# First block row tile by row tile, conditioning summed on VectorE, weights packed in order of use

## The chip, the core and the metric

The kernel runs on one core of a Trainium2 chip. The metric is the time of one execution on the device in microseconds; several runs are made, and their median counts. TensorE multiplies matrices from SBUF into PSUM, VectorE (DVE), ScalarE (ACT) and GpSimd (POOL) work on tiles of 128 partitions, and SyncE (SP) issues the transfers.

## The reference, cut to what matters

Two layers over 512 tokens of width 1024, each with a token mixer and a gated FFN. Every sub-layer is conditioned on a vector `c`:

```python
cs = jax.nn.silu(c)
for layer in range(DEPTH):
    mod = jnp.matmul(cs, ada_w[layer]) + ada_b[layer]          # 1024 x 6144
    sh_m, sc_m, g_m, sh_f, sc_f, g_f = split(mod, 6)
    h = rmsnorm(x, norm_mix_g[layer]) * (1 + sc_m) + sh_m
    y = even_mixer(h, ...) if layer % 2 == 0 else odd_mixer(h, ...)
    x = x + g_m * y
    h = rmsnorm(x, norm_ffn_g[layer]) * (1 + sc_f) + sh_f
    x = x + g_f * conv_glu_ffn(h, ...)
return rmsnorm(x, final_g)
```

The even mixer projects h by a 1024 x 3584 matrix into HGRN2 heads and stick-breaking heads, the odd one by 1024 x 3088 into mLSTM heads, and each has an output projection. Everything is float32.

## The kernel before

x lies transposed in SBUF, 8 row tiles of 128 features by 512 tokens. Each weight and each activation is split into two rounded parts (hi and lo), and a product is three matmuls: hi by hi, hi by lo, lo by hi (`mm3`). `load_split` issues one transfer per weight block from the weight as it lies in memory, casts it to hi on ScalarE and subtracts on VectorE for lo.

Conditioning: `ada_chunk` handles 512 columns of `ada_w` at a time. Its 1024 rows come in four pieces of 512 KB; VectorE multiplies each 128 rows by their value of `cs` and adds them up (8 operations over 128x512). `ada_close` then transposes the sum on TensorE (four transposes, 128x128) and VectorE sums it over the partitions. All chunks but the first four, which the first block handles on its own, are spread over later stages by generators (`ada_many`).

First block (`even_layer`, L536 on): the products with columns 3072 to 3584 and 2560 to 2816 of `even_w_in` (6 outputs) are made first, by quarters q of the features (two row tiles each). For a quarter, `conditioning(q)` loads 8 pieces of 256 KB and adds them up with 8 VectorE operations, `conditioned(q)` makes eight small matmuls with a vector of ones, the gains, and `modulate` (two VectorE and one ScalarE operation per row tile) gives h; `w_load` splits the weights, with the subtraction on GpSimd (`pool_lo`). `products(q, pass)` makes the matmuls of one pass.

After the first block, `weave` runs the chains of the heads step by step with dense products (`cover`) between the steps. Norms: `Stat.add` squares each updated row tile on ScalarE and adds the squares on GpSimd; `ssq_of` sums them over the partitions with matmuls by ones, `rstd_of` takes the power on GpSimd and spreads the result with transposes. This is done for each half of the tokens at the end of a sub-layer, inside `halves_out`, whose second half is multiplied while the first half's h is made.

The order on each engine is set by a list scheduler that goes by program order and its own estimates of when an operand is ready; `behind()` holds a small operation behind the last product queued. All tiles of the `work` pool are shared by all stages, 45 of them.

Of the kernel before, what the change touches and what calls it, by code (L numbers as in the profile page):

```python
# [36 lines left out]

@with_exitstack
def trunk(ctx: ExitStack, tc: tile.TileContext, xT, par_d, masks_d, ada_w, even_w_in, even_w_out,
          odd_w_in, odd_w_out, ffn_w_in, ffn_w_out, outT):  # L40
    nc = tc.nc
    NW, NR, NS, NA = 45, 2, 3, 3
# [65 lines left out]
    nc.vector.tensor_mul(cs, cs, pc("c", 0, 8))  # L108

# [7 lines left out]
    # ---------------- conditioning  # L117
    def ada_chunk(layer, cb):
        a = wt("adaacc")
        before = ada_open[:]  # L120
        del ada_open[:]
        for k2 in range(4):
            r = adap.tile([P, 2, T], F32, tag="ada", name=nm("adaraw"))
            nc.sync.dma_start(r, ada_w[layer, k2 * 256:(k2 + 1) * 256, cb * 512:(cb + 1) * 512]
                              .rearrange("(k p) c -> p k c", p=P))
            for i2 in range(2):
                k = k2 * 2 + i2
                if k == 0:
                    nc.vector.tensor_scalar(a, r[:, 0, :], cs[:, 0:1], None, op0=ALU.mult)
                else:  # L130
                    nc.vector.scalar_tensor_tensor(a, r[:, i2, :], cs[:, k:k + 1], a, op0=ALU.mult, op1=ALU.add)  # L131
            if k2 == 3 and before:
                ada_open.extend(before)
                ada_close()
            yield 0
        ada_open.append((layer, cb, a))

    ada_open = []

    def ada_close():  # L140
        while ada_open:
            layer, cb, a = ada_open.pop(0)
            ps = ps_mx()
            for j in range(4):
                nc.tensor.transpose(ps[:, j * P:(j + 1) * P], a[:, j * P:(j + 1) * P], ident)  # L145
            o = layer * 48 + cb * 4
# [4 lines left out]
    def ada_many(layer, chunks):  # L151
        for cb in chunks:
            yield from ada_chunk(layer, cb)
# [977 lines left out]
```

## Time and profile before

| | |
|---|---|
| median of 3 runs | 1317.85 us (1317.41 to 1317.86) |
| span of the profiled execution | 1316.1 us, 16372 instructions |
| median less the span | 1.75 us |
| TensorE busy | 1271.8 us (97%) |
| VectorE busy | 811.6 us (62%) |
| ScalarE busy | 466.6 us (35%) |
| GpSimd busy | 178.1 us (14%) |
| DMA | 162.51 MB, mean 123 GB/s |

The profile covers one execution from its first to its last instruction; the time of a run also holds what lies outside that. A matmul's duration includes its way through the array, so a stream of them starts every 0.23 us or so though each lasts 0.39.

### The profile page before, as it was taken

The numbers are of one execution on the slowest core, as the hardware profiler recorded it, in microseconds if no ns is written. First come the engines' busy times: TensorE is split into PE (matmuls) and PEld (weight loads), VectorE is DVE, ScalarE is ACT, GpSimd is POOL, SyncE is SP. The second block draws the span as 40 slices with busy tenths as digits, with TensorE's granted clock in tenths as the row PEclk, the third lists the DMA queues.
The fourth block names the chain that finished last, engine by engine and source line by source line (L and its number), as shares of the span: only waits on it lengthen the run. The fifth ranks groups of instructions, "written<-read, shape, count | busy, mean of one in ns | idle before, by whom it ended". The sixth has DMA issues, their size and how long they took to land.

```text
span 1316.1 us, 16372 instructions
## 1 busy us (share of the span) xinstructions
PE 1271.8 (97%) x6458; PEld 1053.1 (80%) x6458; DVE 811.6 (62%) x1198; ACT 466.6 (35%) x725; POOL 178.1 (14%) x258
## 2 busy tenths in 40 slices
PE   4899999999999999999999999999999999999997
PEld 3677788889888888888898768778988888888887
DVE  6844368996797368835756865666785435443454
ACT  3354313124432123212245674775532213221321
POOL 1322144414000000000031020113300000000012
PEclk9999999999999999999999999999999999999998
DMA  8741143562476247633433312112152222222221
GB/s 261 254 154 64 64 129 125 164 192 97 140 234 203 95 150 233 201 119 113 152 113 97 127 33 96 65 65 65 65 184 88 97 95 96 96 97 96 80 72 65
DMA packets 132717, 162.51 MB, mean 123 GB/s; under 512 B 4896, under 2 KB 102944, under 8 KB 132640
## 3 DMA queue, kind: packets, MB, share of 16 engines
q1 hardware_dynamic: 132640, 161.46, 37.8%
q8 instruction: 51, 0.84, 0.3%
q14 instruction: 26, 0.21, 0.1%
HBM read 159.35 MB, written 2.10 MB: 123 GB/s over the span
## 4 chain that ended last, share of the span: by engine, by line
PE 86%; DVE 5%; issue 4%; POOL 2%; ACT 2%; DMA 1%; SPq 0%; POOLq 0%; DVEq 0%; ACTq 0%
PE acc L189 19%; PE acc L190 19%; PE acc L191 19%; PE mx L189 5%; PE mx L190 5%; PE mx L191 5%; PE mx L418 2%; PE acc L227 1%; PE acc L225 1%; PE acc L226 1%; PE mx L808 1%; PE mx L834 1%; PE mx L463 1%; POOL sqa L247 1%; PE mx L145 1%
## 5 line engine op out<-in xcount | busy, mean ns | idle before, releaser
L190 PE MATMUL acc<-hl,wah 128*128 128x512 f32 (+1 forms) x384 | 144.2, 377 | 1.1 <-DVE hl L310 1.0
L189 PE MATMUL acc<-hh,wah 128*128 128x512 f32 (+1 forms) x384 | 145.0, 378 | 0.0
L191 PE MATMUL acc<-hh,wgl 128*128 128x512 f32 (+1 forms) x384 | 144.3, 376 | 0.0
L191 PE MATMUL acc<-hh,wal 128*128 128x512 f32 (+1 forms) x384 | 144.1, 376 | 0.0
L189 PE MATMUL acc<-hh,wgh 128*128 128x512 f32 (+1 forms) x384 | 144.1, 375 | 0.0
L190 PE MATMUL acc<-hl,wgh 128*128 128x512 f32 (+1 forms) x384 | 144.0, 375 | 0.0
L178 DVE TENSOR_TENSOR wl<-wraw,wh 128x2048 fp32r<-128x2048 f32 (+1 forms) x41 | 89.9, 2192 | 54.2 <-ACT wh L177 54.2
L177 ACT CAST wh<-wraw 128x2048 fp32r<-128x2048 f32 (+1 forms) x45 | 79.8, 1774 | 104.5 <-PE acc L190 69.7
L189 PE MATMUL acc<-hh,wh 128*128 128x512 f32 x272 | 111.5, 410 | 0.0
L131 DVE SCALAR_TENSOR_TENSOR adaacc<-adaraw,cs,adaacc 128x512 f32<-128x512 f32 x140 | 106.8, 763 | 6.2 <-DMA adaraw<-ada_w 4.2
L190 PE MATMUL acc<-hl,wh 128*128 128x512 f32 x272 | 108.2, 398 | 0.0
L191 PE MATMUL acc<-hh,wl 128*128 128x512 f32 x272 | 108.0, 397 | 0.0
L245 POOL TENSOR_TENSOR sqa<-sq,sq 128x256 f32<-128x256 f32 x8 | 10.9, 1365 | 698.4 <-ACT sq L239 698.4
L190 PE MATMUL mx<-actl,wdh 128*128 128x512 f32 x256 | 101.0, 395 | 0.0
L189 PE MATMUL mx<-acth,wdh 128*128 128x512 f32 x256 | 101.0, 396 | 0.0
L191 PE MATMUL mx<-acth,wdl 128*128 128x512 f32 x256 | 100.9, 394 | 0.0
L177 ACT CAST wgh<-wgraw 128x2048 fp32r<-128x2048 f32 x22 | 42.0, 1908 | 123.6 <-PE acc L190 86.7
L190 PEld LDWEIGHTS acc<-hl,wah 128*128 128x128 f32 x384 | 72.1, 188 | 15.8 <-DVE hl L310 2.0
L190 PEld LDWEIGHTS acc<-hl,wgh 128*128 128x128 f32 x384 | 72.3, 188 | 14.2
L189 PEld LDWEIGHTS acc<-hh,wgh 128*128 128x128 f32 x384 | 72.2, 188 | 14.1
L191 PEld LDWEIGHTS acc<-hh,wgl 128*128 128x128 f32 x384 | 72.1, 188 | 14.0
L191 PEld LDWEIGHTS acc<-hh,wal 128*128 128x128 f32 x384 | 72.1, 188 | 14.0
(267 smaller groups left out, 2686.6 us busy)
## 6 DMA issues: line engine op xcount, KB each, us to landing
adaraw<-ada_w SPq DMA_DIRECT2D x80, 512.0 KB, 4.4
waraw<-ffn_w_in SPq DMA_DIRECT2D x22, 1024.0 KB, 5.1
wgraw<-ffn_w_in SPq DMA_DIRECT2D x22, 1024.0 KB, 5.1
wdraw<-ffn_w_out SPq DMA_DIRECT2D x16, 1024.0 KB, 4.9
wraw<-odd_w_in SPq DMA_DIRECT2D x12, 1024.0 KB, 5.1
wraw<-even_w_in SPq DMA_DIRECT2D x11, 1024.0 KB, 5.1
adaraw<-ada_w SPq DMA_DIRECT2D x32, 256.0 KB, 4.3
wraw<-ffn_w_out SPq DMA_DIRECT2D x10, 768.0 KB, 4.2
```

Source lines behind the costliest of these rows:

```text
L131: nc.vector.scalar_tensor_tensor(a, r[:, i2, :], cs[:, k:k + 1], a, op0=ALU.mult, op1=ALU.add)
L145: nc.tensor.transpose(ps[:, j * P:(j + 1) * P], a[:, j * P:(j + 1) * P], ident)
L177: nc.scalar.copy(hi, raw)
L178: (nc.gpsimd if pool_lo else nc.vector).tensor_sub(lo, raw, hi.bitcast(F32))
L189: nc.tensor.matmul(out, ah, bh, start=start, stop=False)
L190: nc.tensor.matmul(out, ah, bl, start=False, stop=False)
L191: nc.tensor.matmul(out, al, bh, start=False, stop=stop)
L225: nc.tensor.matmul(ps, ah[:, ts], wh[:, k % 4, :], start=(k == 0), stop=False)
L226: nc.tensor.matmul(ps, ah[:, ts], wl[:, k % 4, :], start=False, stop=False)
L227: nc.tensor.matmul(ps, al[:, ts], wh[:, k % 4, :], start=False, stop=(k == KD - 1))
L247: nc.gpsimd.tensor_add(self.acc, self.acc, s)
L418: nc.tensor.matmul(lps[:, c * 64:(c + 1) * 64].rearrange("p (b m) -> p b m", m=m), k[:, s], qu, start=True, stop=True)
```

## The change

The host stores `ada_w` transposed (a row per conditioning column, 1024 long) and writes every weight block, in order of first use, as one contiguous piece with each partition's part in one run. A column tile of the conditioning is then one transfer of 512 KB and one VectorE operation, which multiplies by the vector `cs` (copied to all partitions once, by eight transposes) and sums along the row; there are no more sums over partitions on TensorE. The first block goes by single row tiles: two conditioning column tiles and one weight piece each, the split on ScalarE and VectorE, nothing on GpSimd, and `conditioned` multiplies x by the norm on VectorE and applies gain and shift on ScalarE, twice (rounded and unrounded). `Stat` adds squares on VectorE and leaves the last square to a matmul of its own. The work pool has 43 tiles for 45.

```diff
-    NW, NR, NS, NA = 45, 2, 3, 3
+    NW, NR, NS, NA = 43, 2, 3, 3
...
+    csb = const.tile([P, D], F32, name="csb")
+    for i in range(2):
+        ps = ps_mx()
+        for j in range(4):
+            nc.tensor.transpose(ps[:, j * P:(j + 1) * P], cs[:, i * 4 + j:i * 4 + j + 1].to_broadcast([P, P]), ident)
+        nc.scalar.copy(csb[:, i * T:(i + 1) * T], ps)
...
+    def ada_load(layer, c, tile_):
+        r0 = (layer * 48 + c) * P
+        nc.sync.dma_start(tile_, adaT[r0:r0 + P, :])
+
+    def ada_column(layer, c, tile_):
+        o = layer * 48 + c
+        nc.vector.tensor_tensor_reduce(out=tile_, in0=tile_, in1=csb, scale=1.0, scalar=pc("ada_b", o),
+                                       op0=ALU.mult, op1=ALU.add, accum_out=mod[:, o:o + 1])
+
     def ada_many(layer, chunks):
         for cb in chunks:
-            yield from ada_chunk(layer, cb)
+            for c in range(cb * 4, cb * 4 + 4):
+                r = adap.tile([P, D], F32, tag="ada", name=nm("adaraw"))
+                ada_load(layer, c, r)
+                ada_column(layer, c, r)
+                yield 0
...
+    def load(raw, srcs):
+        o, n = packer.place(srcs)
+        nc.sync.dma_start(raw, wflat[o:o + P * n].rearrange("(p n) -> p n", p=P))
...
-        (nc.gpsimd if pool_lo else nc.vector).tensor_sub(lo, raw, hi.bitcast(F32))
+        nc.vector.tensor_sub(lo, raw, hi.bitcast(F32))
...
-                nc.gpsimd.tensor_add(self.acc, self.first, s)
-            elif self.count < KD or not self.split:
-                nc.gpsimd.tensor_add(self.acc, self.acc, s)
+                    nc.vector.tensor_add(self.sum, first, s)
+                else:
+                    nc.vector.tensor_add(self.sum, self.sum, s)
             else:
                 self.last = s
...
-            self.ps = ssq_of((self.acc, self.last) if self.split else (self.acc,), self.n // P)
+            self.ps = ssq_of((self.sum, self.last), self.n // P)
...
+        def w_load(k):
+            if k % 2 == 0:
+                ws[k] = [wsp.tile([P, 2048], F32R, tag=tag, name=nm("w0"))[:, 0:1536] for tag in ("wh", "wl")]
+            hi, lo = (t[:, k % 2 * 768:k % 2 * 768 + 768] for t in ws[k - k % 2])
+            ws[k, 0] = hi, lo
+            raw = adap.tile([P, D], F32, tag="ada", name=nm("wraw"))[:, 0:768]
+            rows = slice(k * P, (k + 1) * P)
+            load(raw, [w[rows, 3072:3584], w[rows, 2560:2816]])
+            ws[k, 1] = raw
+
+        def w_split(k):
+            (hi, lo), raw = ws[k, 0], ws[k, 1]
+            nc.scalar.copy(hi, raw)
+            nc.vector.tensor_sub(lo, raw, hi.bitcast(F32))
+
+        def ada_pair(k):
+            r = aq[k] = rawp.tile([P, 2048], F32, tag="raw", name=nm("adaraw"))
+            ada_load(0, 8 + k, r[:, 0:D])
+            ada_load(0, k, r[:, D:2 * D])
+
+        def conditioning(k):
+            r = aq[k]
+            ada_column(0, 8 + k, r[:, 0:D])
+            make_affine(0, 0, k, 1)
+            ada_column(0, k, r[:, D:2 * D])
+
+        def conditioned(k):
+            xr = wt("xr")
+            nc.vector.tensor_mul(xr, x[k], rb)
+            h[k] = (wt("hh", dt=F32R), wt("hl", dt=F32R))
+            a, sh = affA[:, 0, k:k + 1], modc(0, 0, k)
+            nc.scalar.activation(h[k][0], xr, AF.Identity, bias=sh, scale=a)
+            nc.scalar.activation(xr, xr, AF.Identity, bias=sh, scale=a)
+            nc.vector.tensor_sub(h[k][1], xr, h[k][0].bitcast(F32))
...
+        ada_pair(0)
+        w_load(0)
+        ada_pair(1)
+        w_load(1)
...
+        rb = rstd_of(ssq_of((xx, sq), NCH), NCH)
+        w_split(0)
+        conditioned(0)
         vps = [ps_acc() for _ in range(NCH)]
         kps = [ps_mx() for _ in range(2)]
...
+        for k in range(KD):
+            products(k, 0)
+            if k + 1 < KD:
+                conditioning(k + 1)
+                w_split(k + 1)
+                conditioned(k + 1)
+            if k + 2 < KD:
+                ada_pair(k + 2)
+                w_load(k + 2)
+            products(k, 1)
+            products(k, 2)
```

## Rows read from the trace of the kernel before

**Rows 1.** The page's first part: TensorE's busy time, share of the span, instructions.
```profile
PE 1271.8 (97%) x6458; PEld 1053.1 (80%) x6458; DVE 811.6 (62%) x1198; ACT 466.6 (35%) x725; POOL 178.1 (14%) x258
```

**Rows 2.** The table of stretches: start and end, length, engines' busy time, clock, DMA.
```profile
0.00:72.00 72.00, 47.19 (x189) 36.21 (x190) 52.90 (x69) 26.24 (x33) 16.47 (x15) 0.98 0.80 257
...
200.00:306.00 106.00, 104.59 (x647) 91.41 (x646) 89.80 (x152) 27.13 (x62) 35.95 (x51) 1.00 0.50 159
306.00:331.00 25.00, 24.35 (x202) 23.71 (x201) 18.77 (x35) 12.39 (x24) 11.94 (x11) 1.00 0.27 86
331.00:640.00 309.00, 309.00 (x1409) 253.19 (x1408) 210.14 (x271) 82.37 (x74) 0.00 (x0) 1.00 0.53 170
640.00:925.00 285.00, 280.96 (x1515) 231.09 (x1514) 177.75 (x328) 160.13 (x307) 55.07 (x101) 1.00 0.25 82
```

**Rows 3.** The timeline of the first block: start, duration, engine, line, operation.
```profile
12.47 1.86 PE L262 MATMUL mx<-ones,sq 128*128 128x1 f32 x8 [12.47 <-DVE sq L596]
...
16.12 1.11 PE L274 MATMUL mx<-ident,nr 128*128 128x128 f32 x4 [1.79 <-POOL nr L270]
...
23.91 3.97 PE L583 MATMUL acc<-wh,hh 128*128 128x512 f32 x8 [3.29 <-ACT hh L309]
...
33.02 3.50 POOL L178 TENSOR_TENSOR wl<-wraw,wh 128x1536 fp32r<-128x1536 f32 x1 [7.04 <-ACT wh L177]
...
33.73 2.80 DVE L163 SCALAR_TENSOR_TENSOR affA<-mod,par 128x2 f32<-128x2 f32 x1
...
71.95 0.39 PE L189 MATMUL acc<-hh,wh 128*128 128x512 f32 x1
```

**Rows 4.** Groups of VectorE instructions by shape, whole span: count, busy, mean ns.
```profile
L178 DVE TENSOR_TENSOR wal<-waraw,wah 128x2048 fp32r<-128x2048 f32 x22 | 50.4, 2290 | 15.8 <-ACT wah L177 15.8
...
L596 DVE TENSOR_TENSOR sq<-sq,sq 128x512 f32<-128x512 f32 x7 | 4.8, 692 | 4.0 <-ACT sq L592 3.4
L498 DVE TENSOR_TENSOR_SCAN pr<-u 128x512 f32<-128x512 f32 x4 | 4.9, 1223 | 8.3 <-POOL u L493 8.3
...
L498 DVE TENSOR_TENSOR_SCAN pr<-u 128x128 f32<-128x128 f32 x4 | 1.7, 425 | 5.6 <-POOL u L493 5.5
```

**Rows 5.** Groups of VectorE instructions, 200 to 306 us, those of the conditioning.
```profile
L131 DVE SCALAR_TENSOR_TENSOR adaacc<-adaraw,cs,adaacc 128x512 f32<-128x512 f32 x35 | 27.6, 789 | 0.6 <-DMA adaraw<-ada_w 0.5
...
L147 DVE TENSOR_REDUCE mod<-mx 128x4 f32<-128x512 f32 x6 | 4.1, 683 | 0.1
...
L129 DVE TENSOR_SCALAR adaacc<-adaraw,cs 128x512 f32<-128x512 f32 x5 | 2.4, 481 | 0.1
...
L149 DVE TENSOR_TENSOR mod<-mod,par 128x4 f32<-128x4 f32 x6 | 0.9, 156 | 0.1
```

**Rows 6.** The timeline of TensorE around the transposes of two conditioning chunks.
```profile
409.86 1.03 PE L145 MATMUL mx<-ident,adaacc 128*128 128x128 f32 x8
410.65 0.48 PE L189 MATMUL mx<-acth,wdh 128*128 128x512 f32 x1
410.97 0.41 PE L190 MATMUL mx<-actl,wdh 128*128 128x512 f32 x1
411.21 0.40 PE L191 MATMUL mx<-acth,wdl 128*128 128x512 f32 x1
```

**Rows 7.** The timeline of TensorE around one norm's sum, 256 tokens.
```profile
309.69 0.50 PE L262 MATMUL mx<-ones,sqa 128*128 128x1 f32 x4
310.06 0.36 PE L189 MATMUL acc<-oah,wh 128*128 128x256 f32 x1
310.26 0.28 PE L190 MATMUL acc<-oal,wh 128*128 128x256 f32 x1
```

**Rows 8.** Groups of ScalarE instructions by shape, 0 to 72 us.
```profile
L309 ACT ACTIVATE hh<-t,mod 128x512 fp32r<-128x512 f32 x8 | 5.6, 719 | 11.8 <-DVE t L307 11.8
...
L177 ACT CAST wh<-wraw 128x2048 fp32r<-128x2048 f32 x2 | 3.8, 1897 | 1.2 <-DMA wraw<-even_w_in 1.2
```

**Rows 9.** The page's transfers: count, KB each, median us from issue to landing.
```profile
wraw<-even_w_in SPq DMA_DIRECT2D x11, 1024.0 KB, 5.1
```

More of the change, by code (lines that the diff above doesn't have):

```diff
@@ L115, in trunk @@
     affA = const.tile([P, 4, KD], F32, name="affA")
[L118 to L146, printed above, removed]
-            nc.vector.tensor_reduce(mod[:, o:o + 4], ps.rearrange("p (j r) -> p j r", j=4), mybir.AxisListType.X,
-                                    ALU.add)
-            nc.vector.tensor_add(mod[:, o:o + 4], mod[:, o:o + 4], pc("ada_b", o, 4))
+    def ada_load(layer, c, tile_):
[5 more added lines that the diff above has]
+                                       op0=ALU.mult, op1=ALU.add, accum_out=mod[:, o:o + 1])
     def ada_many(layer, chunks):
         for cb in chunks:
-            yield from ada_chunk(layer, cb)
+            for c in range(cb * 4, cb * 4 + 4):
[3 more added lines that the diff above has]
+                yield 0
     def modc(layer, part, j):
@@ L258, in ssq_of @@
         ps = ps_mx()
-        with behind():
-            for t in range(nt):
-                for i, s in enumerate(parts):
-                    nc.tensor.matmul(ps[:, t:t + 1], s[:, t * P:(t + 1) * P], ones1, start=(i == 0),
-                                     stop=(i == len(parts) - 1))
+        for i, s in enumerate(parts):
+            with behind():
+                for t in range(nt):
+                    nc.tensor.matmul(ps[:, t:t + 1], s[:, t * P:(t + 1) * P], ones1, start=(i == 0 and t == 0),
+                                     stop=(i == len(parts) - 1), skip_group_check=True)
         return ps
@@ L305, in modulate @@
             n = sl.stop - sl.start
-            t1 = small.tile([P, 512], F32, tag="t1", name=nm("t1"), bufs=3)[:, :n]
+            t1 = small.tile([P, 256], F32, tag="t1", name=nm("t1"), bufs=3)[:, :n]
             nc.vector.scalar_tensor_tensor(t1, x[j][:, sl], affA[:, i, j:j + 1], rb, op0=ALU.mult, op1=ALU.mult)
@@ L323, in halves_out @@
         for hf in range(2):
-            st = hand.st[hf] = Stat(hf * 256, 256, hand.last and hf == 1)
+            st = hand.st[hf] = Stat(hf * 256, 256)
             done = 0
@@ L564, in conditioned @@
-        def conditioned(q):
-            a = aq[q]
-            ps = ps_mx()
-            for j in range(4):
-                nc.tensor.matmul(ps[:, j:j + 1], a[:, j // 2, (j % 2) * P:(j % 2 + 1) * P], ones1, start=True, stop=True)
-            nc.vector.tensor_add(mod[:, 8 + 2 * q:10 + 2 * q], ps[:, 0:2], pc("ada_b", 8 + 2 * q, 2))
-            nc.vector.tensor_add(mod[:, 2 * q:2 * q + 2], ps[:, 2:4], pc("ada_b", 2 * q, 2))
-            make_affine(0, 0, 2 * q, 2)
-            modulate(0, 0, h, rb, slice(0, T), (2 * q, 2 * q + 1))
@@ new lines, in conditioned, with products @@
+        def conditioned(k):
[6 more added lines that the diff above has]
+            nc.vector.tensor_sub(h[k][1], xr, h[k][0].bitcast(F32))
+        def products(k, ps_):
+            wh, wl = ws[k, 0]
+            s0, s1 = (k == 0 and ps_ == 0), (k == KD - 1 and ps_ == 2)
+            act = h[k][1 if ps_ == 1 else 0]
+            wt_ = wl if ps_ == 2 else wh
+            for i in range(6):
+                if i < 4:
+                    nc.tensor.matmul(vps[i], act[:, i * P:(i + 1) * P], wt_[:, 0:512], start=s0, stop=s1)
+                else:
+                    nc.tensor.matmul(kps[i - 4], wt_[:, 512 + (i - 4) * P:512 + (i - 3) * P], act,
+                                     start=s0, stop=s1)
@@ L981, in take @@
             for _ in range(n):
-                if next(side, None) is None:
-                    ada_close()
+                next(side, None)
         def act_a(fi, aps):
```

109 lines of the change are left out of this document (43 added, 66 removed).

## Prediction

> **What bounds the kernel now.** I read the page's head first, then the table of stretches, then the start of the kernel instruction by instruction. TensorE is busy 97% of the span [rows 1]. So a microsecond of TensorE work taken out nearly anywhere is a microsecond gained, and work on the other engines counts only where TensorE waits for it. The stretches show where that is [rows 2]. From 331 to 640 us TensorE is never idle; from 200 to 306 us it lacks 1.4 us of 106, with VectorE at 89.8 us of the same 106. The first 72 us are the exception: TensorE has work for 47 us, VectorE for 53, and DMA is at 80% of its time.
>
> In that first block [rows 3] the norm of the input is ready for its matmul at 12.5 us, the first product starts at 23.91, and the first product of the next block at 71.95. Between lie 144 products (8 row tiles, 3 passes, 6 outputs), which at the pitch of 0.23 to 0.24 us [rows 6] need 34 us. They took 48. The reason stands in rows 3: GpSimd's subtraction for a weight ran from 33.02 to 36.52, and a VectorE operation on 128x2 that started at 33.73 ended at 36.53. It took 2.80 us where small operations take 0.16 (0.9 us for six, [rows 5]). VectorE stood still while GpSimd worked, and it is VectorE that makes h. This repeats for each quarter.
>
> **The change part by part.** The sum is made on the profiled execution: span 1316.1 us. The median of the runs is 1317.85, so 1.75 us lie outside the span, taken as unchanged.
>
> *The first block.* VectorE's new work for one of 8 row tiles: two multiply-and-sum operations over 128x1024, one small one, a weight subtraction over 128x768, a product and a subtraction over 128x512. Two-source fp32 operations take 0.692 us for 512 elements per partition and 2.290 for 2048 [rows 4], so 1.040 ns per element: 0.96 us for 768 and 1.225 for 1024. The multiply-and-sum itself is in no row. The nearest on one side is this 1.225, with no sum; on the other is VectorE's scan, which also carries a value from element to element: 1.223 us for 512 and 0.425 for 128, or 2.08 ns per element, 2.29 us for 1024. I take 1.33, the first plus 0.1 for reading the sum out (a small operation takes 0.16): the sum is never used inside the row, so it is nearer to the plain operation. That gives 2.66 + 0.16 + 0.96 + 0.69 + 0.69 = 5.16 us per row tile, 41.3 for 8. GpSimd has no part in it, so its standstills go.
>
> A rule of the Trainium skill speaks against this: Vector Engine (DVE) Microarchitecture Reference, Points that are easy to get wrong, says that the two-source-with-scalar form halves its rate when both sources are in SBUF and not bf16, since no port is left for the accumulator. The rows contradict it for the form without a sum (0.789 us for 512 elements of two fp32 sources, rows 5, where the 0.692 of rows 4 is the plain two-source price); no row here shows the form with one. By the rule, an estimate from that page, a multiply-and-sum would take about 2.3 us, and the total would be that of the first rival.
>
> VectorE starts on this when the squares are summed. It sums one square less (0.69 [rows 4] and a gap), so some 0.8 us before the 12.47 of rows 3: at 11.6. 41.3 us of work, and 2 us for waits (the first conditioning rows on their way; the last subtraction behind two ScalarE passes of 0.72 us [rows 8]) end at 54.9. The last row tile's second and third pass then take 12 x 0.235 = 2.8 us: 57.7. TensorE could not be much faster: the norm now needs twice the matmuls (16 records of 0.23 us at the pitch of rows 3, 1.9 us more, less the 0.8), so its transposes end near 18.3 where they ended at 17.23; product 0.69, ScalarE 0.72 and gaps put the first product at about 20, and 34 us from there is 54. DMA has 13.7 MB to bring until the last row tile; at the 257 GB/s of rows 2 that is 53 us, for a need at about 48 (VectorE's last two sums). That would cost some 5 us, but the new pieces are 4 and 3 KB long per partition where the old ones were 1 to 2 KB, and fewer issues sit in the queue; a 1 MB transfer lands in 5.1 us [rows 9], and two buffers of pairs, each filled in 5.1 and read in 2.7, allow a pair every 3.9 us and somewhat more for the issues, under the 5.16. I charge nothing and keep 5 for the range. The next block's first weights need one of the two buffers that the conditioning pairs hold; freed near 46, landed near 52, cast in 1.9 [rows 8] and subtracted in 2.3 [rows 4] once VectorE is through with h at 54.9, they are ready at 57.2, on time if VectorE takes them at once; I charge 0.5. So 71.95 becomes 58.2: **-13.8**.
>
> *The other 20 conditioning chunks (80 columns).* Each chunk had four transposes on TensorE. In rows 6 eight of them start at 409.86, the next product at 410.65, and its successor 0.32 later instead of 0.24: 0.87 us for 8. Eighty are 8.7 us, all in stretches where TensorE is full: **-8.7**. VectorE spent in 200 to 306 us 27.6 + 4.1 + 2.4 + 0.9 = 35.0 us for six chunks [rows 5]; 24 sums of 1.33 are 31.9. It gets a little lighter and stays covered by TensorE. The sums use the same buffers and the same points in the program, so DMA is not moved. The broadcast of the conditioning vector (eight transposes, two copies) runs before 12 us, while TensorE has nothing.
>
> *Sums of squares.* Every norm now has two parts per token tile. Four records start at 309.69 and the next product at 310.06, and that one's successor comes 0.20 later where half of the 0.235 would be 0.12: 0.45 us per norm half [rows 7]. Seven of the eight halves had one part: **+3.1**, all on TensorE. The additions (0.43 us each by the slope above) move to VectorE, which has 18.8 us of work in the 25 around a handoff [rows 2]; five or six of them are 2.4 more, and each must wait for ScalarE's square, with the updates and the h of the other half queued behind it, on which TensorE waits. It lost 0.65 us of those 25 before. A gain is possible too, since GpSimd leaves the last sum. Between -0.6 and 2 for each of two such handoffs; I take **+1.0** in all. The tail after the last product loses at most two small records in front of it: nothing.
>
> *Packed weights.* No product waits for a weight after 72 us: 331 to 640 is full with loads at 170 GB/s. Hidden; if that cover were gone it would already show as TensorE idle. It is a gain only through the first block.
>
> *43 work tiles for 45.* In the first layer the accumulators for conditioning (up to two) no longer take tiles; in the mLSTM layer there were none, so it really has two fewer. 640 to 925 us shows 281.0 of 285 busy [rows 2]. A head that gets its tile later leaves TensorE without cover only at the ends. Between 0 and 8; I take **+1.0**.
>
> Sum: -13.8 - 8.7 + 3.1 + 1.0 + 1.0 = -17.4. Span 1298.7, time 1300.45, given as **1300.4**.
>
> **The rivals.**
> 1. *The sums run at the scan's rate* (2.29 us). A row tile costs 7.08 us of VectorE, 8 cost 56.6; from 11.6 with the same 2 and 2.8 the first block ends at 73, 1 us later than now. In 200 to 306 us VectorE's 89.8 becomes 89.8 - 35.0 + 55.0 = 109.8 of 106: it becomes the bound, and since it idled 16 us there in waits, half of which I let stand, TensorE loses some 12. Sum 1 + 12 - 8.7 + 3.1 + 2 = +9.4: **1327**. It decides from about 2.05 us per sum, where the first block gains 2 and that stretch loses 6. For it: a carried value, in the scan's row. Against it: the price of all other two-source rows. 12 in 100.
> 2. *Two work tiles too few.* The mLSTM heads stall on tiles, 5 to 10 us more than charged: **1305 to 1310**. For it: that layer's many long-lived tiles; against it: only 4 us of idle there now. 12 in 100.
> 3. *The first block gains little*, since pairs land late or VectorE, in its queue order, waits for ScalarE in every row tile (two passes of 0.72 us): 1.5 x 7 = 10 of the 13.8 go: **1307 to 1311**. For it: the subtraction needs both passes; against it: the next row tile's sums can stand between. 14 in 100.
>
> **The numbers.** My forecast holds 62 in 100, with 1294 to 1306 as its own range: DMA 5 us and handoffs 1 us worse at one end, sums at 1.225, no idle and handoffs gaining at the other. Rivals 2 and 3 lie inside 1290 to 1313, the first outside. A change of 0.2% (2.6 us) is about what can be told from none. Faster: 0.62 + 0.12 + 0.13 and a few hundredths of the first rival's milder prices, 0.88; within 0.2%: 0.04; slower: 0.08.
>
> **What would show it.** The first product of the second block near 58 us; multiply-and-sum rows of 1.2 to 1.4 us; no VectorE operation of 2 us on 128x2 in the first block; no transposes in the 331 to 640 stretch, which holds the same products in about 5 us less; four more records in seven norms; handoffs with TensorE idle under 2 us. Wrong if the sums take 2 us, if TensorE waits in the first block come once per row tile for ScalarE, or if 640 to 925 gets longer.

## The result and the profile after

The changed kernel takes 1302.37 us (median of 4 runs, 1300.65 to 1306.5) against 1317.63 beside it (4 runs, 1316.48 to 1317.86): a ratio of 0.9889, 95% interval [0.9871, 0.9906]. The forecast was 1300.4, in a range of 1290 to 1313. The profiled execution took 1300.65 with a span of 1298.9, 17.2 us less than before; 17.4 was the forecast sum. By the medians it is 15.3: the profiled execution of the changed kernel is the lowest of its four. That 17.2 and 17.4 agree so well is partly luck: several terms were off, and their errors cancel. All comparisons of places below are of profiled executions.

The page's first part, to be held against [rows 1]:

```profile
PE 1260.6 (97%) x6390; PEld 1045.4 (80%) x6390; DVE 797.7 (61%) x1212; ACT 473.2 (36%) x736; POOL 118.7 (9%) x199
```

The table of stretches, columns as in [rows 2]:

```profile
0.00:72.00 72.00, 55.62 (x226) 43.68 (x227) 55.90 (x93) 39.90 (x53) 6.70 (x17) 1.00 0.83 301
72.00:200.00 128.00, 120.25 (x595) 93.79 (x594) 112.94 (x186) 46.93 (x109) 42.02 (x60) 1.00 0.74 250
200.00:306.00 106.00, 104.11 (x652) 92.46 (x651) 98.62 (x173) 28.45 (x61) 31.57 (x40) 1.00 0.62 203
306.00:331.00 25.00, 25.00 (x209) 24.67 (x209) 19.42 (x38) 12.12 (x22) 1.67 (x1) 1.00 0.23 85
331.00:640.00 309.00, 309.00 (x1342) 250.32 (x1341) 141.03 (x148) 79.92 (x70) 0.00 (x0) 1.00 0.27 93
640.00:925.00 285.00, 280.91 (x1577) 234.20 (x1576) 189.59 (x363) 166.55 (x321) 34.72 (x80) 1.00 0.22 76
```

Two things in it were not forecast. From 306 us on TensorE has no gap left around the handoff (25.00 of 25; it lacked 0.65 before). And VectorE has 112.94 of 128 us from 72 to 200 us, where the kernel before had 62.80, while it falls from 210 to 141 us in 331 to 640: work has moved from there to here. The kernel before, in 72 to 200 us:

```profile
72.00:200.00 128.00, 123.84 (x593) 97.39 (x592) 62.80 (x100) 49.44 (x106) 35.57 (x60) 1.00 0.29 94
```

Fixed stretches slide against a shorter kernel, so I cut the span at the first start of six kinds of product instead: the first product of the block after the first one; the first transpose of the exponentials (`be`); the first transpose of the HGRN2 output (`on`); the first products with `wah`, `gw` and `och`. Lengths in us, of all profiled executions (e1 to e12 are the experiments below):

| kernel | first block | to be | to on | to wah | to gw | to och | to end | span |
|---|---|---|---|---|---|---|---|---|
| before | 71.95 | 11.4 | 130.3 | 103.8 | 400.1 | 150.5 | 448.1 | 1316.1 |
| after | 59.93 | 12.5 | 133.8 | 101.9 | 394.7 | 150.7 | 445.4 | 1298.9 |
| e1 | 59.8 | 12.5 | 132.3 | 102.5 | 395.1 | 150.6 | 445.5 | 1298.3 |
| e2 | 63.8 | 12.5 | 137.4 | 103.1 | 394.8 | 150.7 | 445.5 | 1307.8 |
| e3 | 71.1 | 11.4 | 130.3 | 103.9 | 399.9 | 150.5 | 447.9 | 1315.0 |
| e4 | 71.95 | 12.0 | 135.1 | 101.6 | 397.1 | 150.6 | 449.4 | 1317.8 |
| e5 | 60.4 | 11.3 | 130.3 | 103.9 | 395.7 | 150.6 | 446.7 | 1298.9 |
| e6 | 58.9 | 12.9 | 132.6 | 103.5 | 394.6 | 150.6 | 446.2 | 1299.3 |
| e7 | 57.1 | 11.5 | 130.3 | 104.1 | 395.7 | 150.6 | 447.0 | 1296.3 |
| e8 | 71.1 | 11.4 | 130.2 | 104.3 | 397.5 | 150.8 | 448.7 | 1314.0 |
| e9 | 57.1 | 13.1 | 133.1 | 99.6 | 394.7 | 150.7 | 446.7 | 1295.0 |
| e10 | 62.2 | 11.4 | 130.3 | 103.3 | 395.7 | 150.6 | 446.8 | 1300.3 |
| e11 | 76.4 | 14.4 | 131.8 | 101.9 | 395.9 | 150.8 | 446.8 | 1318.0 |
| e12 | 61.5 | 13.2 | 135.0 | 103.0 | 397.0 | 150.6 | 447.1 | 1307.4 |

Before against after: -12.0 in the first block, +1.1 and +3.5 up to `on`, -1.9 to `wah`, -5.4 to `gw`, +0.2, and -2.7 to the end: -17.2. The kernels e4 and e8 have the first block of before but for small edits, and theirs are 71.95 and 71.1, so 0.8 us there says nothing.

TensorE's granted clock bears on the first column too. In the profiled execution of the kernel before it stood at half (1.2 of 2.4 GHz) from 63.19 to 66.61 us, 1.4 us after TensorE had idled 1.70 us for h. Four products that take 1.09 us at the full clock took 1.91 there, and TensorE had no gap from there to the block's end:

```profile
61.75 2.94 PE L583 MATMUL acc<-wh,hh 128*128 128x512 f32 x8 [1.70 <-ACT hh L309]
64.49 1.91 PE L585 MATMUL mx<-hh,wh 128*128 128x512 f32 x4
...
68.24 1.09 PE L585 MATMUL mx<-hl,wh 128*128 128x512 f32 x4
```

```profile
63.19:66.61 3.42, 3.42 (x9) 0.50 0.86 300
```

Eight products that start 0.43 us apart in place of 0.23 make 1.6 us, an estimate from these rows. So much of the 12.0 is the clock of that one execution and not the change. The changed kernel's profiled execution has no such stretch between 25 and 1294 us. Of the experiments e1 (at 226 us), e2 (60), e3 (41 to 48), e4 (35 and 52), e6 (226), e8 (34), e10 (58) and e12 (232) have one or two, each beginning 0.3 to 1.8 us after an idle of TensorE of 1.1 to 4.4 us; e5, e7, e9 and e11 have none there. Not every such idle is followed by one: the changed kernel's longest wait for `Q`, 1.9 us, is not.

VectorE's timeline of the first block, the norm's end and then two row tiles (start, duration, line; in brackets the idle time and what ended it):

```profile
11.68 1.28 DVE L168 CUSTOM_DVE_ANT_0 adaraw<-adaraw,csb,par 128x1024 f32<-128x1024 f32 x1 [0.73 <-ACT csb L152]
...
17.28 0.69 DVE L597 TENSOR_TENSOR xr<-x,mx 128x512 f32<-128x512 f32 x1 [4.31 <-PE mx L299]
...
17.95 1.28 DVE L168 CUSTOM_DVE_ANT_0 adaraw<-adaraw,csb,par 128x1024 f32<-128x1024 f32 x1
...
42.78 1.27 DVE L168 CUSTOM_DVE_ANT_0 adaraw<-adaraw,csb,par 128x1024 f32<-128x1024 f32 x1
...
43.99 1.28 DVE L168 CUSTOM_DVE_ANT_0 adaraw<-adaraw,csb,par 128x1024 f32<-128x1024 f32 x1
...
45.20 0.68 DVE L602 TENSOR_TENSOR hl<-xr,hh 128x512 fp32r<-128x512 f32 x1
45.80 0.15 DVE L187 SCALAR_TENSOR_TENSOR affA<-mod,par 128x1 f32<-128x1 f32 x1
45.87 0.95 DVE L580 TENSOR_TENSOR w<-wraw,w 128x768 fp32r<-128x768 f32 x1
46.74 0.68 DVE L597 TENSOR_TENSOR xr<-x,mx 128x512 f32<-128x512 f32 x1
47.33 1.28 DVE L168 CUSTOM_DVE_ANT_0 adaraw<-adaraw,csb,par 128x1024 f32<-128x1024 f32 x1
...
54.09 2.29 DVE L201 TENSOR_TENSOR wl<-wraw,wh 128x2048 fp32r<-128x2048 f32 x1 [2.13 <-ACT wh L200]
56.30 0.68 DVE L602 TENSOR_TENSOR hl<-xr,hh 128x512 fp32r<-128x512 f32 x1
```

From 42.78 to 47.33 VectorE does one row tile without a gap: 4.55 us. TensorE's first product started at 20.14 (forecast: about 20):

```profile
20.14 2.07 PE L611 MATMUL acc<-w,hh 128*128 128x512 f32 x4 [2.90 <-ACT hh L600]
```

After its first sum VectorE stood idle twice: 4.31 us, with the first normalized row tile, which has to wait for the norm, ahead of the second sum, which was ready (in e6, where it may, it starts at 12.74); and 2.13 us near the end, behind which the next block's weights (54.09) went ahead of the last h (56.30).

The multiply-and-sum over the whole span (count, busy us, mean ns), and TensorE at the norm that answers to [rows 7]:

```profile
L168 DVE CUSTOM_DVE_ANT_0 adaraw<-adaraw,csb,par 128x1024 f32<-128x1024 f32 x96 | 122.0, 1283 | 10.4 <-DMA adaraw<-adaT 9.5 <-ACT csb L152 0.7
...
L168 DVE DVE_READ_ACCUMULATOR2_ANT mod<- 128x1 f32 x96 | 7.7, 80 | 0.0
```

```profile
299.88 0.50 PE L287 MATMUL mx<-ones,sqa 128*128 128x1 f32 x4
300.24 0.58 PE L287 MATMUL mx<-ones,sq 128*128 128x1 f32 x4
300.69 0.37 PE L212 MATMUL acc<-oah,wh 128*128 128x256 f32 x1
```

A sum is 1.283 us, near the 1.225 of the plain two-source operation; no row answers to the scan's 2.29. The second part of the norm costs 300.69 - 300.24 = 0.45 us, as reckoned.

Where the 80 later sums stand shows when their rows alone are counted by stretch (busy us, count, then clock and the stretch's DMA; first and last start of all 96 were 11.7 and 297.3 us):

```profile
72.00:200.00 128.00, 56.27 (x45) 1.00 0.74 250
200.00:306.00 106.00, 39.11 (x31) 1.00 0.62 203
331.00:640.00 309.00, 0.00 (x0) 1.00 0.27 93
```

All 80 ran before 300 us, though the program asks for 56 of them after the first FFN begins. In the kernel before 136 of the 160 VectorE operations on these rows stood in 200 to 306 us [rows 5] and in 331 to 640. A sum has no operand but a row tile from memory and the copied vector, so the list scheduler saw it ready and pulled it ahead, with its transfer. Before, a chunk also needed a work tile for its accumulator; that this held it back is an argument, which no run tests by itself.

### The profile page after: what moved, and what is told of

It is laid out like the page before. It is cut to its first block, busy times and chain, and to the rows that moved or that the text cites. A ratio compares the mean times of both kernels' runs of the same rounds, so it can differ in the third digit from the quotient of the medians.

```text
span 1298.9 us, 16095 instructions
## 1 busy us (share of the span) xinstructions
PE 1260.6 (97%) x6390; PEld 1045.4 (80%) x6390; DVE 797.7 (61%) x1212; ACT 473.2 (36%) x736; POOL 118.7 (9%) x199
## 4 chain that ended last, share of the span: by engine, by line
PE 81%; issue 7%; DVE 5%; DMA 4%; POOL 2%; ACT 1%; SPq 0%; POOLq 0%; DVEq 0%; ACTq 0%
PE acc L212 19%; PE acc L213 19%; PE acc L214 19%; PE mx L212 5%; PE mx L213 5%; PE mx L214 5%; DMA adaraw<-adaT 2%; DVE adaraw L168 2%; PE mx L443 2%; PE acc L248 1%; PE acc L250 1%; PE acc L249 1%; PE mx L838 1%; PE mx L864 1%; PE mx L287 1%
## 5 line engine op out<-in xcount | busy, mean ns | idle before, releaser
L168 DVE CUSTOM_DVE_ANT_0 adaraw<-adaraw,csb,par 128x1024 f32<-128x1024 f32 x96 | 122.0, 1283 | 10.4 <-DMA adaraw<-adaT 9.5
L200 ACT CAST wh<-wraw 128x2048 fp32r<-128x2048 f32 (+1 forms) x41 | 73.9, 1802 | 70.5 <-PE acc L213 62.7
L201 DVE TENSOR_TENSOR wgl<-wgraw,wgh 128x2048 fp32r<-128x2048 f32 x22 | 50.4, 2291 | 78.2 <-ACT wgh L200 78.2
L212 PEld LDWEIGHTS acc<-hh,wah 128*128 128x128 f32 x384 | 72.2, 188 | 14.5 <-ACT hh L334 0.4
L200 ACT CAST wah<-waraw 128x2048 fp32r<-128x2048 f32 x22 | 42.0, 1909 | 113.9 <-PE mx L213 73.9
```

What stands on the lines that cost most here:

```text
L168: nc.vector.tensor_tensor_reduce(out=tile_, in0=tile_, in1=csb, scale=1.0, scalar=pc("ada_b", o), op0=ALU.mult, op1=ALU.add, accum_out=mod ...
L200: nc.scalar.copy(hi, raw)
L201: nc.vector.tensor_sub(lo, raw, hi.bitcast(F32))
L212: nc.tensor.matmul(out, ah, bh, start=start, stop=False)
```

## The experiments

In each the edit is made in the changed kernel unless another is named.

**e1, squares back on GpSimd.** `Stat` as before the change, with one part per norm but for the last.

```diff
-                    nc.vector.tensor_add(self.sum, self.sum, s)
+                nc.gpsimd.tensor_add(self.acc, self.acc, s)
...
-            self.ps = ssq_of((self.sum, self.last), self.n // P)
+            self.ps = ssq_of((self.acc, self.last) if self.split else (self.acc,), self.n // P)
```

> The changed kernel with the squares added on GpSimd again and one part per norm half (two in the last half only), as in the kernel before; all else as changed. Theory A (the second part is pure TensorE work, the additions are hidden wherever they are): 7 x 0.45 = 3.1 us less, so about 1299.3 where the changed kernel has 1302.4. Theory B (GpSimd in the handoffs costs TensorE what it costs by standing in VectorE's way: 0.65 us idle of 20 to 25 us at two handoffs before, 0.0 after): of the 3.1 about 1.3 is lost again, so 1.8 us faster than the changed kernel, and TensorE idle by some 0.6 us at each of these handoffs. Slower than the changed kernel would mean that the move itself gained.

Measured: 1302.24 us (1299.96 to 1305.99, 5 runs), ratio to before 0.9887 [0.9868, 0.9906]; the changed kernel had 0.9889. No difference to be seen. The waits of TensorE at the handoffs are back (us, times, longest):

```profile
PE acc L213 <- DVE hl L333: 1.0, 2, 0.5
```

So what the second part costs TensorE (seven times 0.45, by rows) is offset within the measurement; 1.0 of it is this wait. The rest I cannot place, since the runs of one kernel spread over 6 us. From `wah` on e1's stretches are as long as the changed kernel's, but its 102.5 from `on` to `wah` holds a half-clock stretch (226 to 230 us) with TensorE full, up to 1.7 us. So theory B's gain of 1.8 us is not ruled out.

**e2, weights unpacked.** Every weight block loaded from its own array, in rows of 1 to 2 KB.

```diff
-        nc.sync.dma_start(raw, wflat[o:o + P * n].rearrange("(p n) -> p n", p=P))
+        for name, i, r0, r1, c0, c1 in srcs:
+            nc.sync.dma_start(r3[:, :, o:o + c1 - c0], dram[name][i, r0:r1, c0:c1].rearrange("(k p) c -> p k c", p=P))
+            o += c1 - c0
```

> The changed kernel with every weight block loaded from the weight as it lies in memory, in runs of 1 to 2 KB, as before; conditioning rows stay transposed. Theory A (the first block goes at VectorE's pace): the first product of the next block stays within 1.5 us of 59.9 us, and the time within 2 us of 1302.4. Theory B (the longer runs bring the data sooner, and the data set the pace): the first block ends 4 us or more later and the time is 1306 or more.

Measured: 1307.7 us (1305.73 to 1309.47, 4 runs), ratio 0.9917 [0.9898, 0.9937]: 5.3 us more, though the intervals overlap. The first block ends 3.8 us later. In VectorE's timeline and TensorE's waits of 15 to 72 us:

```profile
56.37 2.29 DVE L206 TENSOR_TENSOR wl<-wraw,wh 128x2048 fp32r<-128x2048 f32 x1 [3.99 <-ACT wh L205]
58.58 0.68 DVE L607 TENSOR_TENSOR hl<-xr,hh 128x512 fp32r<-128x512 f32 x1
```

```profile
PE acc L616 <- DVE hl L607: 4.4, 1, 4.4
```

The next block's first weight lands later, ScalarE and VectorE take it up in their queue order, and the last h stands behind it. The page has 6.4 us from issue to landing for these 1 MB blocks, where the packed ones took 5.1; unpacked ones took 5.1 in the kernel before [rows 9] and take 5.2 in e10, where the sums' transfers are not pulled ahead. But the clock was at half from 60.01 to 63.42 us: the last twelve products took 4.45 us where the changed kernel's took 2.89. About 1.6 of the 3.8 is that. Theory B holds in its direction and place (3.8 for its 4 or more), and its time came.

**e3, the kernel before with the first block's split on VectorE.**

```diff
-            ws[q] = load_split([w[rows, 3072:3584], w[rows, 2560:2816]], 2, 768, pool_lo=True)
+            ws[q] = load_split([w[rows, 3072:3584], w[rows, 2560:2816]], 2, 768)
```

> The kernel before with one edit: the weight subtraction of its first block on VectorE in place of GpSimd. Theory A (VectorE sets the pace there and stands still behind GpSimd): VectorE gets 4 subtractions of 1.76 us (7.0) and loses the standstills (four small operations of 2.06 us mean, 7.6 over their price, and 2.5 in one sum: 10.1), so the block ends about 3 us earlier, 69 us in place of 71.95, and the time is about 1314.7. Theory B (the arrival of the pieces sets the pace): no change, 71.95 and 1317.6.

Measured: 1315.53 us (1313.67 to 1317.08, 10 runs), ratio 0.9979 [0.9969, 0.9988]. The small operation is short again (see VectorE's timeline), but TensorE still waits for h in 15 to 72 us, 7.5 us where before it was 8.6 (below, e3's line and then that of the kernel before):

```profile
37.01 0.16 DVE L163 SCALAR_TENSOR_TENSOR affA<-mod,par 128x2 f32<-128x2 f32 x1
```

```profile
PE acc L583 <- ACT hh L309: 7.5, 2, 4.5
PE acc L583 <- ACT hh L309: 8.6, 4, 3.3
```

Two waits are left of four, and from 45.0 us on TensorE has no gap to the block's end. The profiled execution ran at half clock from 41.41 to 48.23 us, so its 71.1 can't be set against 71.95 to a microsecond. The standstill that the prediction took for the first block's reason was real. By the medians it is worth 2.4 us of the whole kernel, between the two theories.

**e4, the kernel before with the 80 later columns as sums.** `ada_chunk` and `ada_close` replaced by `ada_column` (shown ahead of the prediction), 43 tiles. The copied vector needs room, so the `t1` tiles of `modulate` have two buffers in place of three.

```diff
-            yield from ada_chunk(layer, cb)
+            for c in range(cb * 4, cb * 4 + 4):
+                r = adap.tile([P, D], F32, tag="ada", name=nm("adaraw"))
+                ada_load(layer, c, r)
+                ada_column(layer, c, r)
+                yield 0
...
-            t1 = small.tile([P, 512], F32, tag="t1", name=nm("t1"), bufs=3)[:, :n]
+            t1 = small.tile([P, 512], F32, tag="t1", name=nm("t1"), bufs=2)[:, :n]
```

> The kernel before with one part of the change: the 80 later conditioning columns as multiply-and-sum on VectorE (first block, weights and norms as before; 43 tiles). Theory A (each transpose cost TensorE 0.109 us and nothing else changes): 8.7 us less, 1308.9. Theory B (the same, but the sums, which no longer wait for a work tile, are queued far ahead of their program place and stand in front of the stick-breaking heads on VectorE, as 52 of them do between 60 and 200 us in the changed kernel): TensorE idles 4 us more between 72 and 200 us, so about 1313. Theory C (transposes lay in gaps): 1317 or more.

Measured: 1320.83 us (1317.18 to 1325.64, 10 runs), ratio 1.0026 [1.0011, 1.004]: slower, with 80 transposes fewer. The time is theory C's, the place theory B's: the table above shows +4.8 from `be` to `on`, where the changed kernel has +3.5. There is also something I had not thought of: TensorE's waits after 306 us hold

```profile
PE acc L177 <- DVE hl L297: 3.1, 2, 1.6
```

where before there was 1.0 for these two. The third `t` of a handoff has no buffer: VectorE's timeline has three in a row at 312.16 us before, two at 311.66 in e8. That is 2.1 us of this kernel, and of e8, which come, by these rows, from my edit and not from the sums.

**e5, sums held late.** Each later sum is ordered behind the VectorE instruction that stands last before it in the program.

```diff
+    def behind_dve():
+        for ins in reversed(nc.cur_bb.bb.instructions):
+            if ins.engine == mybir.EngineType.DVE:
+                return tc.issue_after(ins)
+        return nullcontext()
...
-                ada_column(layer, c, r)
+                with behind_dve():
+                    ada_column(layer, c, r)
```

> Edit: in the changed kernel every one of the 80 later column sums is ordered behind the VectorE instruction that stands last before it in the program, so that the scheduler can no longer pull the sums (and the loads of their row tiles) ahead of the layers they were meant for. Theory A (the hoisting costs: VectorE at 112.9 of 128 us in 72 to 200 us delays the exponentials' companions that TensorE waits for, 6.5 us behind the be tiles): the stretch from the end of the first block to the first ffn product falls from 248.2 to 243 to 244 us, and the time to 1296.5 to 1298.5 us. Theory B (the sums cost VectorE time wherever they stand, and between 320 and 640 us it has its own work to do too): the 4 to 5 us gained before 308 us are given back between 308 and 700 us, whose length rises from 394.7 to 398 or more, and the time stays within 1.5 us of the changed kernel's. Theory C (a sum held in the order of the program makes what stands behind it wait for its row tile): over 1303 us, with VectorE idle on the row tile's DMA.

Measured: 1300.67 us (1299.9 to 1301.1, 4 runs), ratio 0.9871 [0.9857, 0.9884], span 1298.9 as the changed kernel's. The sums alone by stretch now read

```profile
72.00:200.00 128.00, 8.81 (x7) 1.00 0.25 85
200.00:306.00 106.00, 22.97 (x18) 1.00 0.43 148
331.00:640.00 309.00, 59.98 (x48) 1.00 0.52 175
```

From `be` to `on` it takes 130.3 us, exactly that of before: the 3.5 us there were the pulled-ahead sums. TensorE's waits of 72 to 306 us say it too, first those of the changed kernel, then of e5:

```profile
PE mx L530 <- DVE be L525: 6.5, 8, 1.2
PE mx L443 <- DVE Q L673: 1.9, 1, 1.9
```

```profile
PE mx L537 <- DVE be L532: 3.6, 4, 1.4
...
PE mx L481 <- DVE Q L473: 1.6, 1, 1.6
PE mx L504 <- DVE affA L194: 0.6, 1, 0.6
```

But from `on` to `wah` e5 needs 103.9, as before the change with its 24 transposes there. It gains 2.2 us up to `wah` and gives them all back: 1.0 to `gw`, 1.3 to the end. Both theories were half right, in place and not in size. The median is 1.7 us below the changed kernel's, with intervals that overlap.

**e6, the first block's order.** The first normalized row tile behind both sums of row tile 0; the next block's first cast and subtraction behind the last h of ScalarE and VectorE.

```diff
-            nc.vector.tensor_mul(xr, x[k], rb)
+            with tc.issue_after(summed[0]) if k == 0 else nullcontext():
+                nc.vector.tensor_mul(xr, x[k], rb)
...
-        nc.scalar.copy(hi, raw)
-        nc.vector.tensor_sub(lo, raw, hi.bitcast(F32))
+        with held("act"):
+            nc.scalar.copy(hi, raw)
+        with held("dve"):
+            nc.vector.tensor_sub(lo, raw, hi.bitcast(F32))
```

> Edit: in the changed kernel the first normalized row tile is ordered behind both sums of row tile 0, and the next block's first weight cast and subtraction behind the last h tiles of the first block, on ScalarE and VectorE. Theory A (the 4.3 us idle of VectorE ahead of the norm and the 1.3 and 0.6 us that TensorE waits for the last h tiles are on the path): the first block ends at 55 to 57 us in place of 59.93, and the time is 1297 to 1299 us. Theory B (the chain of row tiles isn't VectorE's but the loads', 1 MB of weights and 1 MB of row tiles in the same 60 us): the first block ends at 58.5 to 60 us, and the time is within 1 us of the changed kernel's. Theory C: what the last weights of the next block lose by being cast later comes out again as a wait of the first products there, so that the block's end moves and the first ffn product (308.1) doesn't.

Measured: 1300.93 us (1300.12 to 1301.85, 4 runs), ratio 0.9873 [0.9858, 0.9888]. The block's products were done at 56.7 us, as theory A wanted, but the next ones did not start. TensorE's timeline there, and ScalarE's:

```profile
56.12 0.63 PE L623 MATMUL mx<-hh,w 128*128 128x512 f32 x2
58.93 0.49 PE L219 MATMUL acc<-hh,wh 128*128 128x512 f32 x1 [2.19 <-ACT vb L567]
```

```profile
56.50 1.90 ACT L206 CAST wh<-wraw 128x2048 fp32r<-128x2048 f32 x1 [2.04 <-DMA wraw<-wflat]
58.30 2.04 ACT L567 COPY vb<-acc 128x512 f32<-128x512 f32 x4
```

The next product needs an accumulator, which is free after ScalarE's copy `vb`; the copy stood behind a cast, and the cast behind a weight still on its way. The end is theory B's, the reason neither's. Theory C's sign is there too: the first FFN product starts at 307.9, in the changed kernel at 308.1; but a half-clock stretch at 226 us stands in between.

**e7, both orders** (e5 and e6 together).

> Edit: both the sums held in the order of the program and the first block's order of the two other kernels of this batch, in the changed kernel. If the two causes are independent, as theory A of both says: first block's end 55 to 57 us, 243 to 244 us from there to the first ffn product, and 1292 to 1295 us. Rival: the weights of the next block and the sums share ScalarE, VectorE and the DMA queue just there, and the gains overlap: 1296 to 1299 us.

Measured: 1298.6 us (1297.63 to 1299.37, 4 runs), ratio 0.9855 [0.9842, 0.9869]. The first block ends at 57.1: with the sums' transfers not pulled ahead, ScalarE's two casts run as one row of 3.70 us from 52.88, and `vb` follows at 56.48. `wah` starts 5.1 us earlier than in the changed kernel; 2.6 remain at the end of the span. The time is the rival's. All its runs lie below the changed kernel's lowest.

**e8, e4 with its sums held late** (the edit of e5).

> Edit: the kernel before with the 80 later columns as VectorE sums (1320.8 us without more) and these sums held in the order of the program. Theory A (what turned 80 fewer transposes into a loss is the hoisting of the sums): the stretch from the end of the first block to the first ffn product falls from 248.75 to 243 to 244 us, and the time to 1308 to 1313 us, the 8.7 us of the transposes' removal visible in full or in half. Theory B (the transposes had filled gaps of TensorE, and their removal is worth little wherever the sums stand): 1316 to 1321 us, with TensorE's idle time in 200 to 640 us larger than before by what the transposes took.

Measured: 1316.38 us (1314.77 to 1319.33, 11 runs), ratio 0.9995 [0.9986, 1.0004]. The expected stretch came back from e4's 248.7 to 245.9 only (11.4 + 130.2 + 104.3), and the 8.7 us are not there: the time is theory B's. The rows say why: 24 transposes stood in 200 to 306 us, 2.6 us, and there TensorE now waits for `Q`, `affA` and `ST`, 3.0 us, where before all its waits made 1.1:

```profile
PE mx L443 <- DVE Q L435: 2.0, 2, 1.6
PE mx L466 <- DVE affA L157: 0.6, 1, 0.6
PE mx L412 <- DVE ST L423: 0.4, 1, 0.4
```

The other 56 transposes (6.1 by [rows 6]) show from `wah` to the end as 1.7, or 3.8 with the 2.1 that the buffers of e4 cost there; what became of the remaining 2 us I cannot say.

**e9, sums spread.** In e7, the 24 sums of layer 0 moved from the second half of the first sublayer to between its earlier weight pieces.

```diff
             yield from fm_piece(w, 2048, h, keep(qs, 0, "qb"))
+            yield from ada_many(0, (4,))
             yield from fm_piece(w, 2816, h, keep(ks, 2, "kb"))
+            yield from ada_many(0, (5,))
...
-            yield from ada_many(0, (8, 9))
```

> Edit: the kernel with both orders (1298.6 us), and in it the 24 sums of layer 0 that its program has in the second half of the first sublayer (200 to 272 us, where VectorE runs without a break from 212 to 267 us) moved to between the earlier weight pieces, 72 to 200 us, where VectorE is busy 70.8 of 128 us. Theory A (16 sums of 1.28 us on a VectorE that is full there hold back what TensorE waits for, 1.8 + 0.6 + 0.6 us, and so take back what 24 fewer transposes give): the stretch from the first on transpose to the first ffn product falls from 104.1 to 101 to 102 us, that before it stays within 1 us of 130.3, and the time is 1295 to 1297 us. Theory B (any sum between the exponentials costs, as the 45 there in the changed kernel did with 3.5 us): the first of these stretches rises by 1.5 us or more, and the time is 1298 us or more.

Measured: 1296.8 us (1296.52 to 1299.47, 5 runs), ratio 0.9841 [0.9828, 0.9854], the lowest of all, though its runs overlap with e7's. The whole table of stretches, 72 to 306 us:

```profile
72.00:200.00 128.00, 121.79 (x603) 95.50 (x602) 86.04 (x138) 46.10 (x107) 44.05 (x62) 1.00 0.43 148
200.00:306.00 106.00, 105.98 (x678) 94.85 (x677) 67.85 (x125) 32.55 (x68) 26.74 (x38) 1.00 0.21 70
```

With VectorE at 67.85 us TensorE fills the second stretch entirely, and `on` to `wah` falls by 4.5 us. But `be` starts 1.6 us later and the stretch behind it is 2.8 longer: +4.4. From the first block's end to `wah` it is 245.8 us, in e7 245.9. So the sums cost TensorE the same in either half; both theories see their own half come true. The time is theory A's.

**e10, unpacked and held late** (e2 and e5 together).

> Edit: the kernel with the sums held late (1300.7 us), and its weights loaded from the separate arrays again, in rows of 1 to 2 KB. Without the packing the changed kernel took 5.3 us more, 3.8 of them in the first block and 4.8 between it and the first ffn product. Theory A (those 4.8 us came from the collision of short runs with the row tiles of the sums that were pulled ahead to 72 to 300 us): with the sums held late only the first block is longer, 63 to 65 us, the stretch after it stays at 245.5 us, and the time is 1303 to 1306 us. Theory B (short runs make weights late in 72 to 300 us by themselves): the stretch after the first block rises by 2 us or more, and the time is over 1306 us.

Measured: 1303.1 us (1302.04 to 1304.19, 4 runs), ratio 0.9884 [0.987, 0.9897]. Behind the first block's end at 62.2 the stretch to `wah` is 245.0 us: theory A. Packing is worth 2.4 us by the medians here (the intervals of this and of e5 overlap, their runs do not), and 5.3 with the sums pulled ahead. The first block of the profiled execution is 1.9 us longer than e5's, but that one ran at half clock from 58.22 to 61.63 us: its last twelve products took 4.45 us, as in e2. That short runs hurt more where they meet another stream of transfers fits the medians and the landings of 6.4 and 5.2 us.

**e11, the sum's price doubled.** An additional multiplication by ones ahead of each sum; it changes no value.

```diff
+        nc.vector.tensor_mul(tile_, tile_, ones1.to_broadcast([P, D]))
         nc.vector.tensor_tensor_reduce(
```

> Edit: in the changed kernel an additional multiplication of the row tile by ones, 128x1024, ahead of each of the 96 sums, which puts some 1.2 us of VectorE time on every column: what the first rival of the prediction (sums at half rate) would have been. Theory A (the first block's pace is VectorE's, 4.55 us per row tile with two sums of 1.28 in it): each row tile takes 2.4 us more, the first block ends at 77 to 80 us, and with the later sums, pulled ahead to a VectorE that is busy 112.9 of 128 us there, the time is 1325 us or more. Theory B (VectorE only follows loads and TensorE in the first block): it ends before 70 us, and the time stays under 1312 us.

Measured: 1320.13 us (1319.01 to 1320.49, 10 runs), ratio 1.0016 [1.0007, 1.0025]. The first block ends at 76.4, 16.5 later. TensorE's waits there (15 to 72 us):

```profile
PE acc L612 <- ACT hh L601: 16.9, 8, 6.1
```

Eight waits, one per row tile: the block's pace is VectorE's. But from there to `wah` it takes 248.1 us, the changed kernel's 248.2. VectorE is fuller (124.76 of 128), yet 63 of the 192 multiplications and sums now stand in 331 to 640, where the changed kernel has none: they could not be pulled ahead so far. Theory A is right on the first block (76.4, just under its 77 to 80), and 5 us too high in the sum.

**e12, 45 tiles.** `NW` 45 in place of 43.

> Edit: the changed kernel with 45 work tiles in place of 43. Theory A (the two tiles are missed nowhere: no wait for a free tile shows in its trace, and 640 to 925 us was no longer than before): within 1 us of the changed kernel, 1300.5 to 1303 us, with the same segments within 0.5 us. Theory B, the prediction's (1.0 us for 43 tiles): 0.8 to 1.5 us faster, with the gain between 700 and 860 us.

Measured: 1304.99 us (1304.65 to 1309.13, 5 runs), ratio 0.9907 [0.9893, 0.9921]: 2.6 us more than the changed kernel's median, with intervals that overlap; its profiled run is the slowest of its five, and its 103.0 from `on` to `wah` holds a half-clock stretch at 232 us. From `gw` to `och` nothing moved (150.6), so the forecast cost of 43 tiles falls. That more tiles are worse neither theory has, and the runs don't settle it; the first block and the stretch from `be` to `on` are the longer ones, and the waits for `hh` (3.7 us) and `be` (7.1) are in kind those of the changed kernel. A scheduler that gets tiles earlier could pull ahead further; no run tests whether it does here.

## Why the prediction was right, step by step

**The first block: -12.0 for -13.8, or -10.4 without the half clock in the kernel before; the mechanism right in the main.** VectorE sets the pace (e11). Its price per row tile was forecast as 5.16 us and the durations of its rows do add up to 5.17 (1.27 + 1.28, two reads of 0.08, 0.68 + 0.15 + 0.95 + 0.68); but each starts some 0.07 us before the record of the last one ends, and a row tile takes 4.55. That is 4.9 us too much over eight. The 2 us for waits were too few by about as much and more: 4.31 idle behind the norm, 2.13 idle and 2.21 of the next block's weights ahead of the last h. This last was seen ("ready at 57.2, on time if VectorE takes them at once") and not drawn to its end: to take them at once is to let the last h wait. e7 runs the second sum ahead of the norm and the last h ahead of those weights; with 3.38 and 1.74 us of idle left at the two places its block ends at 57.1, below the forecast 58.2. The reason given for the slow first block of before, GpSimd's standstills, was the smaller part of it: 2.4 us by the medians (e3). The packing is another part (e2). What single row tiles and what sums along the row are worth no run separates.

**Full rate of the sum.** 1.283 us for the 1.33 taken. The first rival falls: two fp32 sources in SBUF and a running sum did not halve the rate. The rule of the Trainium skill (Vector Engine (DVE) Microarchitecture Reference, Points that are easy to get wrong) thus gives no price for this operation, which the trace lists as CUSTOM_DVE_ANT_0 and not under the two-source-with-scalar form that the rule is about. Had the rate been halved, e11 shows that the price would have been near 1320 and not 1327: the 12 us reckoned for 200 to 306 us did not come, since sums move away from a full VectorE.

**The 80 transposes: mis-sized.** 8.7 us were counted "all in stretches where TensorE is full". From `wah` to `gw` that holds in the main: 48 transposes of 0.109 make 5.2, and it is 5.4 less. With the sums at their place (e5) it is 4.4 less, which is what the transposes, the 0.6 us of idle at the handoff that went and three second parts of 0.45 that came add up to. In e8 it is 2.6 less, with 1.6 us more of idle. For the 24 in 200 to 306 us it does not: TensorE lacked only 1.4 us of 106 there, but VectorE stood at 89.8 and was next. With the sums at their old place nothing of the 2.6 us is left (e5, e8).

**"The sums use the same buffers and the same points in the program, so DMA is not moved": the step that failed.** The points in the program are not points in time. All 80 sums ran before 300 us, at 250 GB/s in 72 to 200 where it was 94, and cost 4.6 us up to `on`. e5 takes these back to the microsecond. Their being gone from `on` on is worth 4.2 us there (e5 against the changed kernel), 2.0 of it up to `wah`, so little is lost in the end: the spans of both are 1298.9. That is luck: the forecast had neither the loss nor the gain.

**Squares and handoffs.** Forecast +3.1 and +1.0. The 0.45 per part stands in the rows; the handoffs gained 1.0 instead of losing it, as the waits show. e1 finds no net difference in the time.

**43 tiles.** Forecast +1.0, measured nothing from `gw` to `och`; the second rival falls. The third, a first block that gains little, also: VectorE never waited once per row tile.

**Packed weights.** "A gain only through the first block" holds when the sums stay in place (e10); with the sums pulled ahead it was worth 5.3 us by the medians (e2); the first block of the profiled execution is 3.8 longer, 1.6 of that by the clock.

So the forecast rest, -8.7 + 3.1 + 1.0 + 1.0 = -3.6, was -5.2, and the first block 1.8 worse: they nearly cancel. Without the half clock the first block is 3.4 worse, and the whole about 15.6 (by the medians 15.3).

## What to carry to other kernels

Work freed of its operands can be moved by the scheduler: for an edit that removes a dependence, ask where the instruction goes, not only what it costs. Taking work off a full engine gains only as far as the next engine is not full in the same stretch, so price both there, by stretch. Add up an engine's pace from starts, not durations, and look at what stands in its queue ahead of the last operation that matters. Before you compare a stretch of two executions, read TensorE's granted clock in both.

## What the runs showed that was not expected

VectorE's records overlap: eight of 5.17 us in sum started within 4.55. A transfer's run length was worth 2.4 us or 5.3 by the medians, with the sums' transfers held back or pulled ahead. Two work tiles more made the kernel 2.6 us slower by median, with intervals that overlap. A wait of TensorE of 1.1 to 4.4 us was at times followed by a stretch at half clock, which cost about 1.6 us more where TensorE was full. And one `t1` buffer less cost two handoffs 1.05 us each (3.1 for 1.0).
